# The combination of the attention groups, the split of its result, and the w_oa additions and splits made in two column halves

## The chip, the cores and the metric

The kernel runs on one core of one Trainium2 chip. The time is in device microseconds (us): one launch, from the core's start to its end, the median of several runs. The core has five engines that run side by side, each through its own instructions in order: PE (TensorE, the matrix products, with the weight loads PEld beside it), DVE (VectorE), ACT (ScalarE), POOL (GpSimd) and SP, which only issues DMAs in this kernel. A product lies in PSUM until another engine has read it; all else lies in SBUF or in DRAM.

## What is computed

One layer of a decoder trunk for 1024 prompt rows and 32 sample rows, 1056 columns in the kernel, which holds everything transposed (features on the 128 partitions, rows of the sequence along the columns). The part that matters here is the middle of the layer: three groups of attention heads are combined by softmax weights, the result goes through w_oa, a gated product, an addition to the other branch, and w_out.

```python
def combine_groups(outs, lses):
    w = jax.nn.softmax(jnp.stack(lses, axis=-1), axis=-1)
    o = jnp.sum(jnp.stack(outs, axis=-2) * w[..., None], axis=-2)
    return o.reshape(*o.shape[:-2], ATT_OUT_W)
...
    att = combine_groups(outs, lses).astype(h.dtype)
    yb, vrows = sgu_branch(uv, sgu_ln_g, sgu_ln_b, sgu_ws, sgu_b)
    mix = (jax.nn.sigmoid(ga) * (att @ w_oa) + jax.nn.sigmoid(gb) * (yb @ w_ob)) @ w_out
    h = layer_norm(ALPHA * h + mix, ln2_g, ln2_b)
    h = layer_norm(ALPHA * h + 0.5 * swiglu(h, f2_w1, f2_w3, f2_w2), ln3_g, ln3_b)
```

`att` has 256 features, `yb` 512, `mix` 1024. Before and behind this part stand two large feed-forward blocks, which take most of the time and which the change does not touch.

## The kernel before

**Products.** Every large product is made three times (`mm3`): an operand x is split into a rounded high part and the rest (`split`: an ACT cast for the high part, a DVE subtraction for the low one, lines 252 and 253), and hi·hi, hi·lo and lo·hi are added up in PSUM. A block is 128 output features by 264 columns (C); the 1056 columns are four blocks, c = 0 to 3. Of the PSUM banks three carry the tag `mm`. Each block in the part around the change takes one of the three, and the bank comes free when DVE has multiplied the block into its place (line 1581, in `product`; I call this the clearing of a block). So PE can be two to three blocks ahead of DVE and then stands.

**The stage.** `mix` (from line 1564) first makes `local(n)` for n = 0 to 5: block row n of the w_ob product, four blocks of 12 matmuls, each cleared by a DVE multiplication with a gate. Meanwhile generators run in the background: `attend` (scores, softmax, values), after it `combine` for head pair 0 and then 1, and `sample_join`, which combines the three groups for the 32 sample rows. Then `split_att` splits the two attention tiles, and the loop over n = 0 to 7 makes the w_oa products: four blocks of 6 matmuls each, cleared the same way, then the addition of both branches (line 1688), then the split of the sum into `m2[n]`, with the last `local` calls and three gates put between. Last comes w_out, whose block (0, c) needs all eight `m2`.

**Combination.** `combine` works out three rows of weights, writes them to DRAM (`cD`, line 1354), and loads each one back, spread over 64 partitions per head (`load`, line 1350, two DMAs for one weight tile `cb`). The loop at line 1358 then multiplies each group's tile by its weights (line 1361) and adds it up (line 1363), whole tiles of 1024 columns on DVE.

**What sets the order.** The code is only the order of recording. A scheduler that simulates the engines decides in which order the instructions stand on each engine, so that a changed duration can move instructions that the diff does not name. A DMA waits in SP's queue behind the DMAs ahead of it, and a DVE instruction behind the DVE instructions ahead of it, whatever it needs itself.

Names in the profile: S, M, W, R, Q are pools of SBUF tiles (W holds split weights, R raw weights), `mm` and `ax` PSUM, `cD`, `jD`, `hD`, `zD` DRAM scratch. jD carries the sample rows' partial results to `sample_join`, hD the residual that w_out's blocks are added to, ws and st are a copy of a state that SP issues piece by piece. L109 on POOL is a one-column copy with which a fresh tile is taken.

## Time and profile before

| What | before |
|---|---|
| median of 3 runs | 2155.13 us |
| the runs | 2155.13, 2155.13, 2161.53 us |
| the profiled execution | 2158.47 us |
| its span (first to last instruction) | 2156.7 us |
| PE busy in the span | 2124.5 us |
| DVE busy | 1552.1 us |
| ACT busy | 889.5 us |
| POOL busy | 323.5 us |
| mean granted clock of PE | 0.995 |

The span is the time from the first to the last instruction of the profiled execution; 1.8 us lie around it (2158.47 less 2156.7). An engine's busy time is the union of its instructions. Times in the views below are microseconds from the start of the span. In a timeline a row gives start, length, engine, line, operation, tiles and sizes, the count of merged instructions, and in brackets how long the engine stood idle before it and what ended that.

### The profile page before, as it was taken

Reading aid. Unit: us, or ns where it says so; the run is one execution under the profiler, and the core shown is the slowest. Engines: PE = TensorE matmul, PEld = TensorE weight load, DVE = VectorE, ACT = ScalarE, POOL = GpSimd, SP = SyncE. Lnnn points to the kernel's source line nnn. Section 1 sums busy time; section 2 is a strip of 40 time slices with the busy share of each in tenths; the row PEclk is TensorE's granted clock in tenths of the full one; section 3 lists DMA queues with packets and bytes.
Section 4 is the critical chain, followed back from the end, with each engine's and each line's share of the span. In section 5 each row is a group of like instructions: output and inputs, shape, how many; then the busy total and the mean of one; then the engine's idle time right before and its main releaser. Section 6 shows DMA issues by size and latency. Waiting matters only on the chain.

```text
span 2156.7 us, 43261 instructions
## 1 busy us (share of the span) xinstructions
PE 2124.5 (99%) x17307; PEld 2086.6 (97%) x17307; DVE 1552.1 (72%) x2727; ACT 889.5 (41%) x1680; POOL 323.5 (15%) x249
## 2 busy tenths in 40 slices
PE   9999999999999999999999999999999999999997
PEld 8999999999999999999988889999999999999997
DVE  8876767747789834887766758787667767657887
ACT  5444444422124644334375544264444444421224
POOL 0432322200000012223000000000323333100000
PEclk9999999999999999999999999999999999999998
DMA  4444545598884335676865755423454544596852
GB/s 154 146 139 170 184 164 169 190 345 311 326 327 167 130 113 174 196 237 207 281 220 164 230 176 189 154 100 119 140 178 149 190 165 159 194 408 267 310 185 81
DMA packets 168378, 426.51 MB, mean 198 GB/s; under 512 B 24353, under 2 KB 59793, under 8 KB 165489
## 3 DMA queue, kind: packets, MB, share of 16 engines
q1 hardware_dynamic: 167744, 423.21, 56.4%
q8 instruction: 135, 2.21, 0.4%
q10 hardware_dynamic: 432, 0.54, 0.1%
q14 instruction: 67, 0.54, 0.1%
HBM read 304.31 MB, written 165.57 MB: 218 GB/s over the span
## 4 chain that ended last, share of the span: by engine, by line
PE 85%; DVE 5%; DMA 5%; issue 1%; POOL 1%; ACT 1%; SPq 1%; ACTq 0%; DVEq 0%; POOLq 0%
PE ax L241 44%; PE mm L241 37%; DMA M<-kv 2%; PE ax L1205 1%; DVE W L253 1%; PE ax L1252 1%; DMA R<-wz 1%; PE ax L1229 1%; DVE M L1428 1%; DMA S<-zD 1%; DMA S<-cD 1%; DVE X L1433 0%; DVE S L631 0%; DMA S<-hD 0%; PE ax L620 0%
## 5 line engine op out<-in xcount | busy, mean ns | idle before, releaser
L241 PE MATMUL mm<-S,W 128*128 128x264 f32 x5400 | 715.7, 287 | 7.9 <-ACT S L252 2.6
L241 PE MATMUL ax<-S,W 128*128 128x264 f32 x5400 | 706.7, 284 | 0.7 <-ACT S L1033 0.5
L241 PEld LDWEIGHTS mm<-S,W 128*128 128x128 f32 x5400 | 677.6, 189 | 21.6 <-issue 8.5
L241 PEld LDWEIGHTS ax<-S,W 128*128 128x128 f32 x5400 | 676.3, 188 | 3.5 <-ACT S L1033 1.7
L241 PE MATMUL ax<-S,S 128*128 128x264 f32 x3240 | 475.7, 284 | 1.8 <-ACT S L1033 1.7
L241 PEld LDWEIGHTS ax<-S,S 128*128 128x128 f32 x3240 | 427.7, 188 | 2.4 <-ACT S L1033 1.9
L241 PE MATMUL mm<-S,S 128*128 128x264 f32 x2280 | 359.6, 286 | 2.7 <-DVE S L924 2.7
L241 PEld LDWEIGHTS mm<-S,S 128*128 128x128 f32 x2280 | 311.3, 189 | 4.1 <-ACT M L593 2.2
L252 ACT CAST W<-R 128x256 fp32r<-128x256 f32 (+2 forms) x175 | 130.7, 764 | 309.3 <-PE mm L241 140.1
L385 POOL TENSOR_TENSOR Q<-R 128x512 f32<-128x512 f32 x49 | 69.9, 1428 | 797.7 <-DMA R<-w13b 219.9
L253 DVE TENSOR_TENSOR W<-R,W 128x256 fp32r<-128x256 f32 (+2 forms) x175 | 156.8, 899 | 22.4 <-ACT W L252 21.4
L252 ACT CAST W<-Q 128x1024 fp32r<-128x1024 f32 (+1 forms) x78 | 76.8, 984 | 218.6 <-POOL Q L386 88.0
L819 DVE SCALAR_TENSOR_TENSOR S<-ax,S 128x264 f32<-128x264 f32 x240 | 99.3, 427 | 66.8 <-PE ax L241 66.4
L461 DVE TENSOR_TENSOR S<-ax,M 128x264 f32<-128x264 f32 x82 | 32.6, 432 | 148.7 <-PE ax L241 148.7
L253 DVE TENSOR_TENSOR S<-Q,S 128x1024 fp32r<-128x1024 f32 (+1 forms) x78 | 111.3, 1427 | 5.5 <-ACT S L252 5.4
L109 POOL CAST S<-ones 128x1 fp32r<-128x1 f32 x36 | 13.6, 384 | 676.0 <-PE ax L241 414.0
L253 DVE TENSOR_TENSOR W<-Q,W 128x1024 fp32r<-128x1024 f32 (+1 forms) x78 | 90.3, 1158 | 29.0 <-ACT W L252 28.9
L252 ACT CAST S<-Q 128x1024 fp32r<-128x1024 f32 (+1 forms) x78 | 76.7, 984 | 67.8 <-PE ax L241 47.2
L253 DVE TENSOR_TENSOR S<-S,M 128x528 fp32r<-128x528 f32 x72 | 83.9, 1165 | 3.7 <-ACT M L252 2.4
L386 POOL TENSOR_TENSOR Q<-Q,R 128x512 f32<-128x512 f32 x49 | 82.7, 1688 | 2.7
L252 ACT CAST S<-R 128x512 fp32r<-128x512 f32 (+1 forms) x62 | 41.9, 676 | 94.2 <-DMA sumsA<-S 39.6
L393 POOL TENSOR_TENSOR Q<-R,Q 128x512 f32<-128x512 f32 x49 | 80.2, 1637 | 1.2
(209 smaller groups left out, 2051.1 us busy)
## 6 DMA issues: line engine op xcount, KB each, us to landing
ws<-st SPq DMA_DIRECT2D x144, 256.0 KB
S<-sumsA SPq DMA_DIRECT2D x63, 528.0 KB
S<-sumsB SPq DMA_DIRECT2D x63, 528.0 KB
M<-kv SPq DMA_DIRECT2D x96, 256.0 KB
sumsA<-M SPq DMA_DIRECT2D x90, 264.0 KB
sumsB<-M SPq DMA_DIRECT2D x90, 264.0 KB
R<-w13b SPq DMA_DIRECT2D x44, 512.0 KB
R<-w13a SPq DMA_DIRECT2D x42, 512.0 KB
```

The source lines that it names most:

```text
L241: mm = lambda a, b, s, e: nc.tensor.matmul(o, a[:, cc], b, start=s, stop=e, skip_group_check=True)
L252: a = self.nc.scalar.copy(hi, src)
L253: b = self.nc.vector.tensor_tensor(lo, src, hi.bitcast(F32), op=ALU.subtract)
L385: tt(s12[:, lo], cd[:, lo], cd[:, hi], op=ALU.add)
L386: tt(s12[:, hi], s12[:, lo], ab[:, lo], op=ALU.subtract)
L393: tt(s34[:, hi], ab[:, hi], s12[:, hi], op=ALU.subtract)
L461: go(one, 5, False, lambda x: tt(h[:, x, 1], one[x], p7[:, x], op=ALU.add))
L819: nc.vector.scalar_tensor_tensor(y(x, r, e), bank[x], HALF, y(x, r, e), op0=ALU.mult, op1=ALU.add)
L1205: nc.tensor.matmul(pS[h][:, r, :nk], q[e, i * P : (i + 1) * P], k[e, k0 : k0 + nk], start=True, stop=True)
L1229: nc.tensor.transpose(pT[r][:, h, o], s[:, r, h, o], self.ident)
L1252: nc.tensor.matmul(pv[0][e, (i % 4) * P : (i % 4 + 1) * P], V[:, i - (nb - 1) + b, e], sT[:, r, h, b * P : b * P + P], start=b == 0, stop= ...
L1428: nc.vector.tensor_tensor(t, t, p.unsqueeze(1).to_broadcast(t.shape), op=ALU.mult)
```

## The change

Three edits, all to operations on whole columns. In `combine` the multiplication and the addition are made in two instructions each, columns 0 to 511 and 512 to 1023. In `split_att` the 1024 prompt columns are split in two halves. In the w_oa loop the addition and the split are made as two halves of 528 columns, each half added and then split; the two tiles of `m2` are taken ahead of the addition. No matmul, no DMA and no tile is added or left out.

```diff
@@ combine
         for g in range(3):
             aT = self.attT.pop((hp, g))
             load(g + 2)
-            nc.vector.tensor_tensor(aT, aT, cbs.popleft(), op=ALU.mult)
-            if g:
-                nc.vector.tensor_tensor(att[:, :NP], att[:, :NP], aT, op=ALU.add)
+            cb = cbs.popleft()
+            for o in (slice(0, 512), slice(512, NP)):
+                nc.vector.tensor_tensor(aT[:, o], aT[:, o], cb[:, o], op=ALU.mult)
+            for o in (slice(0, 512), slice(512, NP)) if g else ():
+                nc.vector.tensor_tensor(att[:, o], att[:, o], aT[:, o], op=ALU.add)
             yield
@@ split_att
-                for o in (slice(0, NP), slice(NP, NT)):
+                for o in (slice(0, 512), slice(512, NP), slice(NP, NT)):
                     self.split(h[:, o], l[:, o], self.att[hp][:, o])
@@ the w_oa loop of mix
-            nc.vector.tensor_tensor(mt[n], mt[n], ta[n], op=ALU.add)
             m2.append((self.S([P, NT], F32R), self.S([P, NT], F32R)))
-            self.split(*m2[n], mt[n])
+            for o in (slice(0, NT // 2), slice(NT // 2, NT)):
+                nc.vector.tensor_tensor(mt[n][:, o], mt[n][:, o], ta[n][:, o], op=ALU.add)
+                self.split(*(x[:, o] for x in m2[n]), mt[n][:, o])
```

The scheduler's order moves with it. In the changed program the lines behind line 1363 have other numbers: 1361 is now 1363, 1363 is 1365, and 1448, 1452, 1581, 1645 and 1647 are each two higher; 1688 is 1692.

**DVE, the combination of head pair 1.** First the order before, from the subtraction of a w_ob weight (L253 on W) on. L1581 clears a block, L1361 and L1363 are the combination, L1459, L1461 and L1464 belong to `sample_join`.

```order
L253 TENSOR_TENSOR W_15517<-R_15516,W_15517 128x512
L1459 TENSOR_SCALAR X_15497<-M_15392,X_15489 128x64
L1581 TENSOR_TENSOR S_15104<-S_15104,mm_15522 128x264
L1461 SCALAR_TENSOR_TENSOR X_15497<-M_15392,X_15489,X_15497 128x64
L1361 TENSOR_TENSOR S_15061<-S_15061,S_15298 128x1024
L1461 SCALAR_TENSOR_TENSOR X_15497<-M_15392,X_15489,X_15497 128x64
L1581 TENSOR_TENSOR S_15104<-S_15104,mm_15536 128x264
L1361 TENSOR_TENSOR S_14348<-S_14348,S_15302 128x1024
L1464 COPY X_15497<-X_15497 128x64
L1581 TENSOR_TENSOR S_15104<-S_15104,mm_15550 128x264
L1363 TENSOR_TENSOR S_15061<-S_15061,S_14348 128x1024
L1581 TENSOR_TENSOR S_15104<-S_15104,mm_15564 128x264
```

And the changed program, from the last clearing ahead of the same subtraction on (S_15107 is the row of blocks that S_15102 was, S_15109 the row that S_15104 was).

```order
L1583 TENSOR_TENSOR S_15107<-S_15107,mm_15512 128x264
L253 TENSOR_TENSOR W_15527<-R_15526,W_15527 128x512
L1363 TENSOR_TENSOR S_15066<-S_15066,S_15303 128x512 x2
L1583 TENSOR_TENSOR S_15109<-S_15109,mm_15532 128x264
L1363 TENSOR_TENSOR S_14348<-S_14348,S_15307 128x512 x2
L1583 TENSOR_TENSOR S_15109<-S_15109,mm_15546 128x264
L1365 TENSOR_TENSOR S_15066<-S_15066,S_14348 128x512
L1583 TENSOR_TENSOR S_15109<-S_15109,mm_15560 128x264
L1365 TENSOR_TENSOR S_15066<-S_15066,S_14348 128x512
L1363 TENSOR_TENSOR S_14724<-S_14724,S_15329 128x512 x2
L1454 TENSOR_REDUCE X_15500<-M_15402 128x1
L1583 TENSOR_TENSOR S_15109<-S_15109,mm_15574 128x264
```

The first multiplication by the weights now stands one clearing earlier: before, block 0 of the row S_15104 was cleared ahead of it, now its counterpart comes behind it. `sample_join`, whose first instruction is L1454 (1452 before), has moved from ahead of the combination into it.

**SP, the loads of the same combination.** Before:

```order
L1438 DMA jD<-X_13031 128x66
L1448 DMA M_15392<-jD 64x66 x2
L231 DMA R_15578<-wo 128x512
L1354 DMA cD<-S_14961 16x128 x3
L1350 DMA S_15298<-cD 64x1024 x2
L1350 DMA S_15302<-cD 64x1024 x2
L231 DMA R_15650<-wo 128x512
L1350 DMA S_15324<-cD 64x1024 x2
```

And the changed program:

```order
L1440 DMA jD<-X_13031 128x66
L1450 DMA M_15402<-jD 64x66
L231 DMA R_15588<-wo 128x512
L1354 DMA cD<-S_14966 16x128 x3
L1350 DMA S_15303<-cD 64x1024 x2
L1350 DMA S_15307<-cD 64x1024 x2
L1350 DMA S_15329<-cD 64x1024
L231 DMA R_15660<-wo 128x512
L1350 DMA S_15329<-cD 64x1024
L1450 DMA M_15402<-jD 64x66
```

The last load of jD, which `sample_join` needs, now goes behind all the weight loads of the combination; one half of the third weight tile goes ahead of a w_ob load.

**DVE, the start of the w_oa loop.** L1647 (1649) is a row sum of a w_out tile, L1470 (1472) puts the sample rows into the attention tiles, L253 on W is the low part of the first two w_oa weights. Before:

```order
L1647 TENSOR_REDUCE X_15604<-Q_15606 128x8
L1581 TENSOR_TENSOR S_15232<-S_15232,mm_15701 128x264
L253 TENSOR_TENSOR W_15716<-R_15715,W_15716 128x256
L1581 TENSOR_TENSOR S_15721<-S_15721,mm_15748 128x264
L1581 TENSOR_TENSOR S_15721<-S_15721,mm_15756 128x264
L1581 TENSOR_TENSOR S_15721<-S_15721,mm_15764 128x264
L1581 TENSOR_TENSOR S_15721<-S_15721,mm_15772 128x264
L253 TENSOR_TENSOR W_15740<-R_15739,W_15740 128x256
L1688 TENSOR_TENSOR S_14895<-S_14895,S_15721 128x1056
```

And the changed program:

```order
L1649 TENSOR_REDUCE X_15614<-Q_15616 128x8
L1583 TENSOR_TENSOR S_15237<-S_15237,mm_15711 128x264
L1472 COPY S_13970<-ax_15608 64x32 x2
L1472 COPY S_15066<-ax_15608 64x32 x2
L253 TENSOR_TENSOR W_15726<-R_15725,W_15726 128x256
L253 TENSOR_TENSOR S_15738<-S_13970,S_15737 128x32
L253 TENSOR_TENSOR S_15746<-S_15066,S_15745 128x32
L1583 TENSOR_TENSOR S_15731<-S_15731,mm_15762 128x264
L1583 TENSOR_TENSOR S_15731<-S_15731,mm_15770 128x264
L1583 TENSOR_TENSOR S_15731<-S_15731,mm_15778 128x264
L1692 TENSOR_TENSOR S_14900<-S_14900,S_15731 128x528
L1583 TENSOR_TENSOR S_15731<-S_15731,mm_15786 128x264
```

The copies and splits of the sample rows, done long before in the old order, now stand directly around the low part of the first w_oa weight; the addition's first half stands ahead of the fourth clearing.

## The prediction

> **What bounds the kernel now.** I read the page first, then PE's own timeline through the stage of the change, then DVE and SP beside each gap that PE shows there. The first part of the page settles the scale:

> ```profile
> PE 2124.5 (99%) x17307; PEld 2086.6 (97%) x17307; DVE 1552.1 (72%) x2727; ACT 889.5 (41%) x1680; POOL 323.5 (15%) x249
> ```

> PE is busy 2124.5 us of a span of 2156.7 us, and the change takes no matmul away. It can win only stalls of PE, 32 us in the whole kernel, and of these only the ones in its own stage. PE's timeline from the last `local` rows to the first w_out block:

> ```profile
> 1263.08 22.10 PE L241 MATMUL mm<-S,W 128*128 128x264 f32 x180
> 1286.59 1.70 PE L241 MATMUL mm<-S,W 128*128 128x264 f32 x12 [1.40 <-DVE S L1581]
> 1288.83 0.30 PE L1467 MATMUL ax<-ident,X 128*128 128x128 f32 x1 [0.54 <-DVE X L1464]
> 1289.07 3.19 PE L241 MATMUL mm<-S,W 128*128 128x264 f32 x24
> 1292.91 1.74 PE L241 MATMUL mm<-S,W 128*128 128x264 f32 x12 [0.65 <-DVE S L1581]
> 1295.44 6.09 PE L241 MATMUL mm<-S,W 128*128 128x264 f32 x48 [0.79 <-DVE S L253]
> 1302.07 35.27 PE L241 MATMUL mm<-S,W 128*128 128x264 f32 x282 [0.54 <-ACT W L252]
> 1337.80 19.03 PE L241 MATMUL mm<-S,W 128*128 128x264 f32 x150 [0.46 <-DVE S L1581]
> 1357.22 2.96 PE L241 MATMUL mm<-S,W 128*128 128x264 f32 x22 [0.38 <-DVE S L1707]
> ```

> The brackets are the stalls: 1.40 + 0.54 + 0.65 + 0.79 + 0.54 + 0.46 + 0.38 = 4.76 us. The unstalled rate is 22.10 / 180 = 0.123 us per matmul, so 12 matmuls (one block of `local`) take 1.47. From 1302.07 to 1356.83 PE makes 432 matmuls in 54.76 us, where 432 x 0.123 is 53.1: some 1.7 us of stalls, 0.46 of them in a bracket, the rest too short for one. What holds PE at 1286.59 stands on DVE:

> ```profile
> 1279.39 0.43 DVE L1581 TENSOR_TENSOR S<-S,mm 128x264 f32<-128x264 f32 x1 [0.25 <-PE mm L241]
> 1280.86 0.42 DVE L1581 TENSOR_TENSOR S<-S,mm 128x264 f32<-128x264 f32 x1
> 1284.68 1.23 DVE L1361 TENSOR_TENSOR S<-S,S 128x1024 f32<-128x1024 f32 x1 [3.20 <-DMA S<-cD]
> 1286.02 0.42 DVE L1581 TENSOR_TENSOR S<-S,mm 128x264 f32<-128x264 f32 x1
> 1287.35 1.23 DVE L1361 TENSOR_TENSOR S<-S,S 128x1024 f32<-128x1024 f32 x1 [0.91 <-DMA S<-cD]
> 1288.60 0.42 DVE L1581 TENSOR_TENSOR S<-S,mm 128x264 f32<-128x264 f32 x1
> 1290.69 1.23 DVE L1361 TENSOR_TENSOR S<-S,S 128x1024 f32<-128x1024 f32 x1 [0.20 <-DMA S<-cD]
> 1292.43 0.42 DVE L1581 TENSOR_TENSOR S<-S,mm 128x264 f32<-128x264 f32 x1
> 1294.87 0.43 DVE L1581 TENSOR_TENSOR S<-S,mm 128x264 f32<-128x264 f32 x1
> ```

> L1361 at 1284.68 waits 3.20 us for its weights, and the next clearing waits behind it until 1286.02. PE had filled its three banks at 1263.08 + 22.10 = 1285.18 and stood until that clearing ended. The gaps at 1292.91 and 1295.44 end with the clearings of 1292.43 and 1294.87, which stand behind whole-tile operations. So what bounds this stretch is DVE's order around three arrivals of weights, 1284.68, 1287.35 and 1290.69, which the halves do not bring forward.

> **The price of a half.** A whole operation beside two halves of the same size:

> ```profile
> L1361 DVE TENSOR_TENSOR S<-S,S 128x1024 f32<-128x1024 f32 x6 | 7.4, 1226 | 8.0 <-DMA S<-cD 8.0
> 1215.18 1.28 DVE L1428 TENSOR_TENSOR M<-M,X 128x512 f32<-128x512 f32 x2
> L1688 DVE TENSOR_TENSOR S<-S,S 128x1056 f32<-128x1056 f32 x8 | 10.0, 1251 | 0.0
> ```

> Two of 512 take 1.28 us in a row, one of 1024 takes 1.23: a cut costs 0.05. The diff adds 28 DVE instructions (6 + 4 in the combination, 2 in `split_att`, 8 additions, 8 low parts), 1.4 us of DVE in all, and ten ACT casts. A clearing that comes just behind a started operation waits 0.6 us in place of 1.2.

> [...]

> **The combination of head pair 1, step by step.** The order moves L1361 (1363 now) ahead of one clearing, the one that stood at 1280.86. PE fills its banks one block sooner, at 1285.18 - 1.47 = 1283.71. Against that, the small operations of `sample_join` and its transpose on PE (the 0.54 gap) move behind, and the operations are halves. I take the arrivals 0.3 us later (the instructions ahead of L1341, which makes the weights, stand in another order; bounds 0 and 0.7, one weight subtraction more ahead of it, 676 ns in the rows below), 0.6 for a half, 0.4 for a clearing to its end, and 0.05 until PE goes on:

> - Weights at 1285.0, two halves, clearing ended 1286.6; PE restarts at 1286.65, a stall of 2.9 in place of 1.4, one block behind the old order.
> - Second weights at 1287.65, two halves, clearing ended 1289.25; PE at 1289.3. Behind it half an addition and a clearing, ended 1290.2, so the next block follows at once at 1290.75.
> - Half an addition, third weights at 1291.0, two halves, L1454, clearing ended 1292.75; PE at 1292.8.
> - A subtraction for a weight, half an addition, clearing ended 1294.3; PE at 1294.35 until 1295.8. Half an addition and two clearings are through by 1295.7; the last row of `local` runs without a stall, 48 matmuls, 1295.8 to 1301.7.

> Before, the same point is 1295.44 + 6.09 = 1301.53. So the block that is lost first is won back: **+0.2 us**. If nothing is won back it is +1.5; if the clearings slip in better than I count, the gaps 0.54 + 0.65 + 0.79 go too and it is -2.0.

> What must hold for this is that L1454 does not wait, for it now stands ahead of a clearing. Its operand comes by the last jD load:

> ```profile
> 1275.01 1.10 SPq L1448 DMA_DIRECT2D M<-jD  x2
> 1278.27 0.15 DVE L1452 TENSOR_REDUCE X<-M 128x1 f32<-128x3 f32 x1
> 1279.32 2.76 SPq L1350 DMA_DIRECT2D S<-cD  x4
> 1282.81 1.08 SPq L1350 DMA_DIRECT2D S<-cD  x2
> 1283.30 7.27 DMA S<-cD
> ```

> SP issues the last weights from 1283.30 on, and they land 7.27 us later. The last jD load goes out behind them, about 1284.0. With the 3.3 us that it took before (1275.01 to 1278.27) it is there at 1287, with 7.27 at 1291.3; L1454 is reached at 1292.2. So nothing, on the dearer row with 0.9 us to spare.

> **The start of the w_oa loop.** Its first weight takes the slot of the last `local` weight, an ACT cast (1301.61, the 0.54 us gap), and that stays. New is that the low part of this weight stands on DVE behind the copies of the sample rows:

> ```profile
> L1470 DVE COPY S<-ax 64x32 f32<-64x32 f32 x4 | 0.7, 187 | 0.1
> L1647 DVE TENSOR_REDUCE X<-Q 128x8 f32<-128x1024 f32 x5 | 6.1, 1211 | 0.0
> L253 DVE TENSOR_TENSOR W<-R,W 128x512 fp32r<-128x512 f32 x8 | 5.4, 676 | 0.2 <-ACT W L252 0.2
> 1301.61 0.40 ACT L252 CAST W<-R 128x256 fp32r<-128x256 f32 x1 [1.61 <-issue]
> ```

> PE has six matmuls (0.74 us) with the high part before it needs the low one. The transpose follows the last `local` block at 1301.7, the copies take 4 x 0.187 = 0.75 from about 1302.0, the subtraction 0.4: ready at 1303.2, needed at 1302.2 + 0.74 = 1302.95. **+0.3 us**, bounds 0 and 1.3 (a row sum of 1.21 that starts just before).

> **The w_oa blocks.** DVE is nearly full here (start and end, length, then busy time of PE, PEld, DVE, ACT and POOL, the granted clock, DMA):

> ```profile
> 1303.00:1338.00 35.00, 34.54 (x278) 33.82 (x277) 30.75 (x54) 13.79 (x20) 0.00 (x0) 1.00 0.58 189
> ```

> DVE is busy 30.75 of 35 us, PE 34.54. The 1.7 us of short stalls are clearings behind a row sum, an addition or a subtraction; halves cut the wait behind the latter two. Half of 1.7 would be -0.85; 16 cuts at 0.05 add 0.8 us of DVE and give some back. I take **-0.5 us**, bounds -1.7 and +0.8. ACT's casts in halves and two more table loads have cover: ACT is busy 13.79 of these 35 us. A table load is 1.28 us and stands on ACT where it idles for 5.21 and 7.31:

> ```profile
> 1285.27 0.62 ACT L252 CAST W<-R 128x512 fp32r<-128x512 f32 x1 [5.21 <-PE mm L241]
> 1293.19 0.22 ACT L252 CAST S<-S 128x32 fp32r<-128x32 f32 x1 [7.31 <-DVE S L1470]
> 1297.62 1.28 ACT L1684 ACT_TABLE_LOAD   x1 [1.18 <-DMA S<-zD]
> ```

> I cost them at 0; without that cover they would hold a weight's cast for up to 2.6 us.

> **The first w_out block and head pair 0.**

> ```profile
> 1350.31 0.33 SPq L220 DMA_DIRECT2D R<-wout  x1
> 1351.25 4.34 SPq L279 DMA_DIRECT2D S<-hD  x8
> 1356.73 0.43 DVE L1707 SCALAR_TENSOR_TENSOR S<-mm,S 128x264 f32<-128x264 f32 x1 [2.88 <-DMA S<-hD]
> 1212.83 0.44 PE L1229 MATMUL ax<-ident,S 128*128 128x128 f32 x2 [1.26 <-ACT S L1233]
> ```

> The hD loads stand in SP's queue behind the w_out load of 1350.31; in the new order one w_out load fewer is ahead of them. The 0.38 us stall at 1357.22 should go in the main: **-0.3 us** (0 to -0.4). The w_out load that goes behind them is for a later unit, and a unit is used for 4 x 24 matmuls, 11.8 us. For head pair 0 the stall of 1.26 ends when a whole multiplication has freed a tile; two halves are 0.05 later each time: **+0.1** (0 to 0.2).

> **The sum.** 0.2 + 0.3 - 0.5 - 0.3 + 0.1 = -0.2 us. On the profiled execution, whose span is 2156.7 us (2158.47 with what lies around it), that is 2156.5; the median of the runs lies 3.3 us under that execution, so I take 2155.13 - 0.2, rounded: **2155.0 us**. The forecast is no change that can be told: a difference under 0.3% (6.5 us) is about what a measurement of this kernel cannot tell from none, and the three runs are themselves 6.4 us apart.

> **The rivals.**

> *All clearings slip in.* The combination's gaps go (-2.0), the short stalls of w_oa (-1.7), 0.38 at w_out, and the 1.40 as well if the old count of clearings ahead of the weights hardly matters: -5.5, 2149.6 us. For it: every one of these gaps ends at DVE. Against it: one clearing fewer stands ahead of the wait, and arrivals set the pace. To pass 6.5 us it needs something outside this stage too.

> *The sample rows come late.* Place: L1454 on DVE, ahead of a clearing. If the last jD load is slower than I count, every microsecond past 1292.2 is one of PE, whose three banks are full. The longest wait for a load in the chain of waits is

> ```profile
> 1064.14 9.92 DMA S<-zD
> ```

> With 9.92 us it lands at 1293.9: +1.7, and with nothing won back in the combination (+1.5), the row sum in the way (+1.3) and a further +0.8 in w_oa 2160.4 us. It decides from a landing at 1292.2 on, and is slower beyond 0.3% from about 1298.5. For it: the load is now the last of its queue's ten rows shown above. Against it: it is 64 x 66 values and took 3.3 us.

> *DVE runs full.* At 88% busy each cut costs its whole fixed part, and the clearings queue. The dear price, the whole of 28 x (2 x 0.674 - 1.226) = 3.4 us by mean lengths, with the 0.5 not won, is 2158.8 us. [...] For it: DVE's 30.75 of 35. Against it: the pair of 512.

> **How the numbers follow.** The forecast has 0.60: 0.56 within the bound, 0.02 on either side by the runs' own spread. All clearings slip in: 0.16, of which 0.11 beyond the bound. Sample rows late: 0.12, 0.07 beyond, since its price is not bounded by a row of the same load. DVE full: 0.12, 0.05 beyond with the spread. Faster 0.02 + 0.11 = 0.13, slower 0.02 + 0.07 + 0.05 = 0.14, the same 0.73. The likeliest case's own range is 2153 to 2157 us from the bounds that add up by chance. The range of 8 in 10 reaches from the first rival, 2150, to the second, 2160.4, and to what a median takes from the upper run: 2150 to 2161.

> **What would show it.** In the changed profile: PE stalls 2 to 3.5 us once near 1284, ended by the clearing behind the first pair of halves (right), or under 1.5 (my count of clearings is wrong); PE begins the w_oa loop within 1 us of 1302; the low part of its first weight ends a PE gap of 0.2 to 0.5; the rows from there to the w_out block take 53.5 to 55 us; the gap ended by L1707 is gone. L1454 shows a DMA as its releaser if the second rival is right. A sum of DVE in the w_oa stretch over 33 of 35 us would speak for the third. The forecast fails if a stall appears in a part that the order leaves alone, or if the runs move as a whole by more than their spread.

## The result, and the profile after

| | before | after |
|---|---|---|
| median | 2156.23 us | 2159.89 us |
| runs | 22, from 2153.85 to 2161.53 | 22, from 2155.36 to 2164.74 |
| ratio | | 1.0014, 95% interval 1.0008 to 1.002 |
| the profiled execution's span | 2156.7 us | 2162.0 us |

The change makes the kernel slower by 0.14%, some 3 us: less than the 0.3% that I took for what can be told, but with 22 runs on either side it can be told. The forecast was no change (2155.0 us). The profiled execution of the changed kernel is the slowest of its 22 runs, so its stalls are larger than usual ones; the repeats below show how much larger.

The first part of the page of the changed kernel:

```profile
PE 2127.2 (98%) x17307; PEld 2089.4 (97%) x17307; DVE 1553.2 (72%) x2755; ACT 893.8 (41%) x1692; POOL 317.9 (15%) x249
```

The matmuls are the same in number, and PE is busy 2.7 us longer. DVE has the 28 instructions more that were counted, for 1.1 us more of busy time where I had worked out 1.4; ACT has two instructions more than the ten casts, the two table loads. PE's timeline through the stage, for the rows from 1263.08 on that were shown of before:

```profile
1264.26 8.97 PE L241 MATMUL mm<-S,W 128*128 128x264 f32 x72
1273.47 11.92 PE L241 MATMUL mm<-S,W 128*128 128x264 f32 x96 [0.24 <-DVE S L1583]
1287.55 2.12 PE L241 MATMUL mm<-S,W 128*128 128x264 f32 x12 [2.16 <-DVE S L1583]
1289.88 12.92 PE L241 MATMUL mm<-S,W 128*128 128x264 f32 x96 [0.22 <-DVE S L1583]
1302.64 0.27 PE L1469 MATMUL ax<-ident,X 128*128 128x128 f32 x1
1303.34 1.01 PE L241 MATMUL mm<-S,W 128*128 128x264 f32 x6 [0.43 <-ACT W L252]
1304.51 11.19 PE L241 MATMUL mm<-S,W 128*128 128x264 f32 x90 [0.16 <-DVE W L253]
1317.91 17.99 PE L241 MATMUL mm<-S,W 128*128 128x264 f32 x132 [2.22 <-DVE S L1583]
1336.32 6.84 PE L241 MATMUL mm<-S,W 128*128 128x264 f32 x54 [0.41 <-DVE S L1583]
1343.40 22.81 PE L241 MATMUL mm<-S,W 128*128 128x264 f32 x181 [0.25 <-DVE S L1583]
```

Up to the w_oa loop it reads as predicted: one long stall behind the first pair of halves (2.16 us), no gaps of 0.54, 0.65 and 0.79 behind it, and the loop begins 39.08 us behind the first `local` row (1303.34 - 1264.26), where before it was 38.99. New is the stall of 2.22 us at 1317.91, which the prediction does not have. Behind it the gap ended by L1707 is gone. Two more things are in the lengths: 12 matmuls take 2.12 us at 1287.55 (1.47 is the full rate), and 132 take 17.99 (16.2). Both rows stand behind a long stall, where the granted clock was 0.50 for 3.41 us. Here are the stretch with the second stall and the one behind it (start and end, length, then busy time of PE, PEld, DVE, ACT and POOL, the granted clock, DMA):

```profile
1315.97:1319.38 3.41, 1.47 (x12) 1.50 (x13) 2.64 (x5) 1.04 (x3) 0.00 (x0) 1.00 0.27 72
1319.38:1322.79 3.41, 3.41 (x17) 3.41 (x17) 3.13 (x7) 1.26 (x2) 0.00 (x0) 0.50 0.75 217
```

What stands ahead of 1317.91 on ACT of the changed kernel:

```profile
1315.12 1.08 ACT L1686 ACTIVATE S<-S 128x1056 f32<-128x1056 f32 x1 [5.85 <-DMA S<-zD]
1316.11 0.91 ACT L252 CAST W<-R 128x512 fp32r<-128x512 f32 x2
```

On its DVE:

```profile
1316.74 0.69 DVE L253 TENSOR_TENSOR W<-R,W 128x512 fp32r<-128x512 f32 x1 [2.77 <-ACT W L252]
1317.35 0.76 DVE L1583 TENSOR_TENSOR S<-S,mm 128x264 f32<-128x264 f32 x2
```

And in SP's queue, the load that the sigmoid needs:

```profile
1308.93 0.58 SPq L1141 DMA_DIRECT2D S<-zD  x1
```

ACT of the kernel before, at the same place:

```profile
1311.10 0.62 ACT L252 CAST W<-R 128x512 fp32r<-128x512 f32 x1 [2.63 <-PE mm L241]
1312.20 1.09 ACT L1684 ACTIVATE S<-S 128x1056 f32<-128x1056 f32 x1 [0.47 <-DMA S<-zD]
```

Read it from the last fence up. Before, ACT casts the last w_ob weight at 1311.10, 9.03 us into the w_oa loop, as soon as PE has left the slot, and then takes the sigmoid of the fifth gate, whose load from zD has just come. After, the two have changed places: ACT waits 5.85 us for that load (issued at 1308.93), and the cast stands behind it until 1316.11, 12.77 us into the loop. DVE waits 2.77 us for the cast, two clearings stand behind DVE's subtraction, and PE behind the clearings. Neither PE nor DVE waits for the sigmoid itself in this loop.

### The profile page after: what moved, and what is told of

Read it like the earlier page. It is cut to its first block, busy times and chain, and to the rows that moved or that the text cites. A ratio compares the mean times of both kernels' runs of the same rounds, so it can differ in the third digit from the quotient of the medians.

```text
span 2162.0 us, 43300 instructions
## 1 busy us (share of the span) xinstructions
PE 2127.2 (98%) x17307; PEld 2089.4 (97%) x17307; DVE 1553.2 (72%) x2755; ACT 893.8 (41%) x1692; POOL 317.9 (15%) x249
## 4 chain that ended last, share of the span: by engine, by line
PE 89%; DVE 4%; DMA 4%; ACT 1%; issue 1%; POOL 1%; SPq 0%; ACTq 0%; DVEq 0%; POOLq 0%
PE ax L241 46%; PE mm L241 38%; PE ax L1205 1%; DMA M<-kv 1%; DMA S<-zD 1%; PE ax L1252 1%; PE ax L1229 1%; DVE W L253 1%; DMA S<-cD 0%; DVE S L253 0%; DVE S L631 0%; DMA R<-wz 0%; DVE S L554 0%; PE ax L620 0%; PE ax L1549 0%
## 5 line engine op out<-in xcount | busy, mean ns | idle before, releaser
L241 PE MATMUL mm<-S,W 128*128 128x264 f32 x5400 | 719.0, 288 | 10.2 <-DVE S L1583 5.5
L241 PE MATMUL ax<-S,W 128*128 128x264 f32 x5400 | 706.6, 284 | 2.2 <-ACT S L1033 2.0
L241 PEld LDWEIGHTS mm<-S,W 128*128 128x128 f32 x5400 | 681.0, 190 | 23.9 <-issue 8.0
L241 PEld LDWEIGHTS ax<-S,W 128*128 128x128 f32 x5400 | 676.1, 188 | 5.0 <-ACT S L1033 3.4
L241 PE MATMUL ax<-S,S 128*128 128x264 f32 x3240 | 475.9, 284 | 2.9 <-ACT S L1033 1.8
L241 PEld LDWEIGHTS ax<-S,S 128*128 128x128 f32 x3240 | 427.6, 188 | 3.8 <-ACT S L1033 2.0
L241 PE MATMUL mm<-S,S 128*128 128x264 f32 x2280 | 359.4, 286 | 2.6 <-DVE S L924 2.6
L241 PEld LDWEIGHTS mm<-S,S 128*128 128x128 f32 x2280 | 311.0, 189 | 3.9 <-issue 2.9
L252 ACT CAST W<-R 128x256 fp32r<-128x256 f32 (+2 forms) x175 | 130.6, 764 | 305.7 <-PE mm L241 126.7
L253 DVE TENSOR_TENSOR W<-R,W 128x256 fp32r<-128x256 f32 (+2 forms) x175 | 155.7, 893 | 25.2 <-ACT W L252 24.1
L252 ACT CAST W<-Q 128x1024 fp32r<-128x1024 f32 (+1 forms) x78 | 76.8, 984 | 222.4 <-POOL Q L386 90.8
L253 DVE TENSOR_TENSOR S<-Q,S 128x1024 fp32r<-128x1024 f32 (+1 forms) x78 | 112.0, 1436 | 5.5 <-ACT S L252 5.5
L253 DVE TENSOR_TENSOR W<-Q,W 128x1024 fp32r<-128x1024 f32 (+1 forms) x78 | 89.9, 1153 | 31.1 <-ACT W L252 31.1
L252 ACT CAST S<-Q 128x1024 fp32r<-128x1024 f32 (+1 forms) x78 | 76.7, 984 | 68.2 <-PE ax L241 50.2
L253 DVE TENSOR_TENSOR S<-S,M 128x528 fp32r<-128x528 f32 x72 | 83.8, 1164 | 2.6 <-ACT M L252 1.0
L252 ACT CAST S<-R 128x512 fp32r<-128x512 f32 (+1 forms) x62 | 41.9, 676 | 99.9 <-DMA sumsA<-S 42.3
L393 POOL TENSOR_TENSOR Q<-R,Q 128x512 f32<-128x512 f32 x49 | 80.7, 1647 | 1.2
```

Source lines behind the costliest of these rows:

```text
L241: mm = lambda a, b, s, e: nc.tensor.matmul(o, a[:, cc], b, start=s, stop=e, skip_group_check=True)
L252: a = self.nc.scalar.copy(hi, src)
L253: b = self.nc.vector.tensor_tensor(lo, src, hi.bitcast(F32), op=ALU.subtract)
L393: tt(s34[:, hi], ab[:, hi], s12[:, hi], op=ALU.subtract)
```

## The experiments

Every comparison has 11 or 12 runs of the kernel against 23 to 35 of the kernel before on the same chip, so a ratio's interval is some 0.0008 to 0.0010 to either side. That is as large as the effect, so I read the traces beside it. In every profile I take three stretches, read at the same matmuls: **L** from the first local row (before: 1263.08) to the first w_oa block (1302.07), **W** from there to the matmul at 1337.80, **T** from there to 1400.09 in the w_out blocks. One table for all, in microseconds (in `after_early` the stall near 1285 is another one: PE's transposition waits there for L1466, a copy of the sample rows):

| kernel | stall near 1285 | granted clock behind it | L | W | T | ratio |
|---|---|---|---|---|---|---|
| before | 1.40 | 1.00 | 38.99 | 35.73 | 62.28 | |
| before_again | 1.12 | 1.00 | 38.04 | 35.59 | 62.67 | 0.9997 |
| comb_alone | 1.09 | 1.00 | 37.56 | 35.69 | 62.70 | 1.0002 |
| before_swap | 1.12 | 1.00 | 38.03 | 37.43 | 62.69 | 1.0008 |
| oa | 1.21 | 1.00 | 38.62 | 36.49 | 61.60 | 1.0001 |
| oa_tied | 1.27 | 1.00 | 38.18 | 35.68 | 61.61 | 0.9994 |
| oa_tied_again | 1.21 | 1.00 | 39.04 | 35.66 | 61.63 | 0.9986 |
| before_stall | 2.28 | 0.50 | 38.52 | 35.51 | 62.71 | 0.9997 |
| before_stall_fill | 1.30 | 1.00 | 38.11 | 36.41 | 62.53 | 1.0004 |
| splitatt_alone | 2.17 | 0.50, twice as long | 40.81 | 36.80 | 62.56 | 1.0006 |
| comb_split | 2.08 | 1.00 | 38.82 | 35.98 | 62.76 | 1.0010 |
| comb_split_again | 1.94 | 1.00 | 38.20 | 36.08 | 62.64 | 1.0012 |
| after_tied | 2.50 | 0.50 | 39.46 | 36.11 | 61.62 | 0.9997 |
| tied_again | 2.57 | 0.50 | 39.20 | 36.12 | 61.60 | 1.0010 |
| after | 2.16 | 0.50 | 39.08 | 40.07 | 61.61 | 1.0014 |
| after_again | 2.03 | 1.00 | 38.27 | 36.57 | 61.61 | 1.0009 |
| after_early | 2.09 | 0.50 | 39.30 | 35.67 | 61.65 | 1.0001 |
| after_late | 3.39 | 0.50 | 40.00 | 37.12 | 61.60 | 1.0007 |
| tied_late | 2.85 | 0.50 | 39.44 | 36.08 | 61.60 | 1.0003 |
| tied_fill | 1.15 | 1.00 | 39.34 | 35.98 | 61.61 | 1.0006 |

### The sigmoid ahead of the cast

Two kernels take the new order out and put it into the old kernel. The first is the changed kernel with the sigmoid issued behind the cast (three neighbours on DVE change places as well):

```diff
-                nc.scalar.activation(ta[n], ta[n], AF.Sigmoid)
+                with self.tc.issue_after(self.cast) if n == 4 else ExitStack():
+                    nc.scalar.activation(ta[n], ta[n], AF.Sigmoid)
```

Here `self.cast` is the cast of the last w_ob weight.

> The changed kernel with one order on ACT put back: the sigmoid of the fifth w_oa gate (n = 4) is issued behind the cast of the last w_ob weight, as before the change; every engine's order is otherwise that of the change but for three neighbouring swaps on DVE. Theory A (the sigmoid waits for its gate's load with the weight's cast queued behind it): PE's 2.2 us stall near 1318 is gone, the stretch from the first w_oa matmul to the first w_out clearing is 3 to 4 us shorter than in the changed kernel, ratio to before 0.999 to 1.0005. Rival B (28 more DVE instructions cost it, or the clearing that the combination lost): the stretch stays, ratio 1.001 to 1.002.

The second is the kernel before, whole operations throughout, with the fifth gate loaded and its sigmoid recorded in `local(6)`, and the last w_ob cast issued behind it:

```diff
+                if n == 6:
+                    early.append(self.fetch_z(30))
+                    sig = nc.scalar.activation(early[0], early[0], AF.Sigmoid).ins
```

> The kernel before, whole tiles everywhere, with that one order changed: the gate's sigmoid (n = 4) ahead of the cast of the last w_ob weight on ACT. Theory A: a PE stall of 1.5 to 3 us appears behind that cast, the sigmoid shows a DMA of zD as its releaser, ratio 1.001 to 1.002. Rival B: no stall, ratio 0.9995 to 1.0005.

Measured: 2156.84 us, ratio 0.9997 [0.9988, 1.0006] without the swap, and 2158.41, 1.0008 [1.0000, 1.0017] for the swap alone. W says the same: it falls from 40.07 to 36.11 without the swap, and rises from 35.6 or 35.7 to 37.43 with it. The stall of PE behind the cast is 0.92 us in `before_swap`, less than the 1.5 to 3 expected. Then the halves of the w_oa loop alone, which bring the swap with them, and the combination with `split_att` alone, which does not:

> Only the w_oa additions and splits in halves; the combination and its split whole. The sigmoid stands ahead of the cast here too. Theory A: the stall of about 2 us in the w_oa loop is there, ratio 1.0008 to 1.002, as the whole change. Rival B in the form of the combination's lost clearing: ratio 0.9995 to 1.0005.

> The combination and the split of its result in halves, the w_oa additions and splits whole. Here the sigmoid stays behind the cast. Theory A: ratio 0.9995 to 1.0005, PE begins the w_oa loop within 0.5 us of the kernel before when counted from the last local rows; no stall over 1 us from there to w_out. Rival B in the form of the lost clearing: 1.5 us later at the w_oa loop, ratio 1.0007 or more.

`oa`: 2156.57, 1.0001 [0.9992, 1.0009], under the 1.0008 or more that the swap was to give: W has the swap (36.49), but T is 1.0 us shorter. `comb_split`: 2159.47, 1.0010 [1.0001, 1.0018], which a swap that explains everything would not give. So the first four kernels show one cost, and that there is another.

The same four parts once more, and a kernel that loads the w_oa gates four ahead in place of three (`ta` begins with four), which puts the sigmoid behind the cast, the sample rows' operations ahead of the combination, and needs no more table loads, with all halves kept:

> The changed kernel itself once more, for a second profile. Theory A (the sigmoid in front of the weight's cast, priced by how late its gate's load lands): the stretch from the first w_oa matmul to the 282nd is as much over 36.1 us as the load of zD lands behind the time at which the weight's slot comes free, somewhere from 0.5 to 4 us; ratio 1.0005 to 1.002. Rival C (the 2.2 us stall of the first profile is a chance of that one execution and the change costs elsewhere): the stretch is at 36.1 and the ratio is still 1.001 or more.

> The changed kernel with the sigmoid behind the cast, once more. Theory A: ratio 0.999 to 1.0003, the stretch 36.0 to 36.3 us. Rival C: ratio 1.001 as the change.

> The combination and the split of its result in halves, once more, since its first ratio of 1.001 does not fit theory A while its profile shows no stall that the kernel before has not. Theory A: ratio 0.9995 to 1.0006. Rival D (the new order of the combination costs by itself, through the lost clearing and two more table loads): 1.0007 to 1.0015 again, and the last local rows or the head pair 0 part 0.7 us or more longer than before in its profile.

> All halves of the change, and each gate of the w_oa loop loaded one block row earlier (four ahead in place of three). The scheduler then puts the sigmoid behind the cast and the sample rows ahead of the combination again, as before the change. Theory A: no stall over 1 us in the w_oa loop, ratio 0.9985 to 1.0000. Rival B (the cuts cost by their number): 1.001 or more.

Measured: 2158.57, 1.0009 [1.0000, 1.0019]; 2158.44, 1.0010 [1.0001, 1.0018]; 2158.71, 1.0012 [1.0003, 1.0021]; 2156.00, 1.0001 [0.9992, 1.0010]. Note `tied_again`: the kernel whose first measurement was 0.9997 is 1.0010 here. One measurement of this size settles nothing. `comb_split_again` repeats the cost, but its profile shows neither longer last local rows (L 38.20) nor a longer head pair 0, as its expectation asked. `after_early` has all the halves, W at 35.67 and a ratio of 1.0001, which speaks against a cost by the number of halves.

SP and then ACT of `after_again` show why the swap's price differs from one execution to the next:

```profile
1304.57 0.58 SPq L1141 DMA_DIRECT2D S<-zD  x1
```

```profile
1308.80 1.09 ACT L1686 ACTIVATE S<-S 128x1056 f32<-128x1056 f32 x1 [3.90 <-DMA S<-zD]
1309.79 0.60 ACT L252 CAST W<-R 128x512 fp32r<-128x512 f32 x1
```

Here the load is there 4.2 us after its issue (1304.57 to 1308.80), in `after` 6.2 us. The cast stands 10.83 us into the loop (1309.79 - 1298.96), 1.8 us later than in its own place, and PE has cover for most of that: its timeline has only a gap of 0.27 there. In `after`, the cast is 3.7 us late and PE stands for 2.22. In W the swap costs 0.5 us (`after_again`), 0.8 (`oa`), 1.0 (`after_late`), 1.8 (`before_swap`) and 4.0 (`after`), against the same order without it: 1.6 on average. Two of these are not the swap alone. In `after`, the 132 matmuls behind the stall take 17.99 us where `after_again` takes 16.43 for the same row, and these 1.56 us are the half clock that followed. In `before_swap`, 0.87 us are the gap ahead of the matmul at which W ends, and that gap is anything from 0.22 to 1.10 us in the kernels with whole w_oa operations. Without `after` the average is 1.0.

### Each edit alone, and no edit

> The kernel before under a name of its own: nothing is changed. It tells how far a kernel without any change may fall from the runs beside it. If the differences of 1.0008 to 1.0012 seen so far come from the changes, this one lies between 0.9995 and 1.0005, and from the start of the stage's last 950 us (PE's block at 1195 us) to the end its trace shows 946 us, as the first trace of before does (946.0). If it falls outside 0.9993 to 1.0007, such differences cannot be told from no change at all, and the theories of a lost clearing and of a late load have nothing left to explain.

> Only the multiplications and additions of combine are halved; split_att and the w_oa loop are as before. The order keeps the first multiplication behind the same clearing, the sample rows' operations ahead of the combination and the sigmoid behind the last weight cast. If the halves in combine are what costs (their own 0.05 us per cut, or the small shifts on PE and ACT in head pair 0), 1.0010. If the cost comes from the order that split_att brings with it, 1.0000, with PE's stall near 1285 still 1.4 us or less.

> Only the split of the attention tiles is made in halves (two casts and two subtractions more); the multiplications are whole. The order puts the first multiplication one clearing earlier, the sample rows' operations behind it, the last load of jD behind the weight loads of the combination, and two more ACT table loads. If this order is what costs, 1.0010 (about +2 us) with a PE stall of 2 to 3 us near 1285. If the order costs nothing and the halves in combine do, 1.0000.

> Only the w_oa blocks' additions and splits are halved, and the sigmoid of the fifth gate is issued behind the cast of the last w_ob weight, as before. If the halves of the w_oa loop win the 0.5 us of the stall ahead of w_out and the swap with the sigmoid was all that they cost, 0.9997, with the stretch from the first w_oa block to the second at 35.7 to 36.1 us. If the swap costs nothing on the whole time, the same as with the swap, 1.0001.

Measured: 2156.74, 0.9997 [0.9989, 1.0006]; 2157.08, 1.0002 [0.9993, 1.0010]; 2158.08, 1.0006 [0.9998, 1.0015]; 2156.28, 0.9994 [0.9986, 1.0002]. The unchanged kernel under another name is off by 0.0003, but the two measurements of `after_tied` and `tied_again` are 0.0013 apart, so a difference of 0.0010 is read only where it repeats over several kernels. The halves in `combine` alone cost nothing that can be told. It is the halves in `split_att`, which no term of my sum named, that bring the new order around the combination: with them alone the first multiplication stands ahead of the clearing, the sample rows behind it, and the stall is 2.17 us. And the w_oa halves, once the swap is out, are a gain. PE of `oa_tied` in the w_oa loop:

```profile
1300.74 28.18 PE L241 MATMUL mm<-S,W 128*128 128x264 f32 x228 [0.54 <-ACT W L252]
1329.33 6.82 PE L241 MATMUL mm<-S,W 128*128 128x264 f32 x54 [0.41 <-DVE S L1581]
1336.42 28.76 PE L241 MATMUL mm<-S,W 128*128 128x264 f32 x230 [0.27 <-DVE S L1581]
```

228 matmuls run without a bracket, 54 and 230 more follow with small gaps ahead of them, and the stall ahead of w_out that ended at L1707 is not there. T is 61.60 to 61.65 in every kernel with these halves, and 62.28 to 62.76 in every one without.

### The stall near 1285, and the clock behind it

The table shows a pattern: where the stall was 2.09 us or longer, the granted clock was 0.50 for the next 3.4 us. Four kernels were to tell whether the second cost is this stall, the half clock, or the sample rows. The first is the kernel before with nothing added but the stall; two instructions change places on DVE:

```diff
+            with self.tc.issue_after(self.first_mult) if held else ExitStack():
                 with self.urgent():
                     nc.vector.tensor_tensor(t[:, cc], t[:, cc], p, op=ALU.mult)
```

`held` is true for block row 3, c = 0, and `first_mult` is the first multiplication of head pair 1.

> The kernel before, in which one clearing and the first multiplication of the second combination change places on DVE (nothing is halved; the multiplication by the first weights is issued ahead of the clearing of block row 3, c = 0). Theory of the clock: PE's stall grows from 1.1 to 1.4 us to about 2.7 us, that is more than half of a stretch of 3.4 us, and in about two of three executions the granted clock is 0.5 in the next 3.4 us; the mean clock over the runs falls by 0.0005 and the time is 1.0007 to 1.0012. Theory of the lost clearing alone: the stall grows as well but is won back within the next blocks, time 1.0000 to 1.0004, mean clock as in the kernel before. Theory of the sample rows (their late operations, the late jD load, two more table loads are what costs): they are untouched here, so 1.0000.

The second fills the stall with nine matmuls that are made twice:

```diff
+            for k, (xh, xl) in enumerate(xs[:fill]):
+                self.mm3(p, wo, k * P, xh[:, cc], xl[:, cc], k == 0, False)
```

> As the run before it, but nine of the twelve matmuls of block row 3, c = 2 are made twice (the first time for nothing, into the same bank), so that PE works 1.1 us of its stall. The scheduler moves three neighbours on DVE and one cast. Theory of the clock: the stall is 1.6 us, under half of a stretch of 3.4 us, the clock stays 1.00, and the kernel is faster than the one with the bare stall by 0.0004 to 0.0008 although it makes more matmuls. Theory of the lost clearing alone, and that of the sample rows: the same time as with the bare stall.

The third and fourth are the changed kernel, and the one without the swap, with the first multiplication put behind that clearing:

> The changed kernel, in which the first multiplication goes back behind the clearing of block row 3, c = 0; all halves, the sample rows' place, the late jD load, the table loads and the sigmoid ahead of the weight cast stay. Theory of the clock and of the clearing: PE's stall near 1285 is 1.1 to 1.4 us again, no half clock there, and 1.0003 (what is left is the sigmoid, about +1.3 us, less what the w_oa halves win, about 1). Theory of the sample rows: as the changed kernel, 1.0010.

> The changed kernel with both orders put back: the first multiplication behind the clearing, the fifth gate's sigmoid behind the weight cast. Theory of the clock, the clearing and the sigmoid together: all that costs is gone, what the w_oa halves win is left, 0.9995. Theory of the sample rows: 1.0005 (about +2 us from them, less 1).

Measured: 2156.41, 0.9997 [0.9988, 1.0005]; 2158.14, 1.0004 [0.9995, 1.0012]; 2159.12, 1.0007 [0.9998, 1.0017]; 2158.20, 1.0003 [0.9994, 1.0011]. PE of `before_stall`, and two of its stretches (start and end, length, then busy time of PE, PEld, DVE, ACT and POOL, the granted clock, DMA):

```profile
1281.14 4.72 PE L241 MATMUL mm<-S,W 128*128 128x264 f32 x24 [2.28 <-DVE S L1584]
1285.70 0.27 PE L1469 MATMUL ax<-ident,X 128*128 128x128 f32 x1
1285.73 10.47 PE L241 MATMUL mm<-S,W 128*128 128x264 f32 x84
1296.74 35.29 PE L241 MATMUL mm<-S,W 128*128 128x264 f32 x282 [0.54 <-ACT W L252]
```

```profile
1278.26:1281.68 3.42, 1.14 (x9) 0.93 (x9) 2.10 (x4) 0.00 (x0) 0.00 (x0) 1.00 1.02 252
1281.68:1285.09 3.41, 3.41 (x18) 3.41 (x18) 3.38 (x6) 0.62 (x1) 0.00 (x0) 0.50 1.03 299
```

The stall is there, the half clock is there, and L is 38.52 all the same, between the two profiles of before. The stall is 0.9 us longer than in the first profile of before, and 24 matmuls take 4.72 us in place of 2.95, but DVE goes on meanwhile, and when the clock is back it is so far ahead that the three gaps are gone and 84 matmuls run in a row. In this profile the lost clearing is won back, as the prediction had it: what the half clock takes, PE would else have stood in the gaps. The time, 0.9997, did not bear out the theory of the clock, which had 1.0007 or more. It does not refute it either: that theory also had the mean granted clock 0.0005 lower, and over the 11 runs it is 0.9955, as in the runs of the kernel before beside them, so the half clock need not have come in most of them. `before_stall_fill` keeps the full clock and has L 0.4 us shorter (38.11), but W is 36.41 and the time 1.0004. The theory of the clock had it faster than the bare stall, and missed.

The third and fourth kernels did not do what they were for; `after_late` shows why. With the first pair of halves behind the clearing, both pairs stand ahead of the next clearing, and PE waits for the second weights in place of the first:

```profile
1273.24 13.40 PE L241 MATMUL mm<-S,W 128*128 128x264 f32 x108 [0.24 <-DVE S L1586]
1290.03 13.46 PE L241 MATMUL mm<-S,W 128*128 128x264 f32 x96 [3.39 <-DVE S L1586]
```

They say only that this one move does not take the stall out of this order.

What the half clock does in the changed order can be read from `after` and `after_again`, one program whose profiles differ in the clock. DVE of `after`, then of `after_again`, at the same clearings:

```profile
1295.03 0.94 DVE L1583 TENSOR_TENSOR S<-S,mm 128x264 f32<-128x264 f32 x2
1299.91 0.43 DVE L1583 TENSOR_TENSOR S<-S,mm 128x264 f32<-128x264 f32 x1 [0.58 <-PE mm L241]
```

```profile
1291.39 0.76 DVE L1583 TENSOR_TENSOR S<-S,mm 128x264 f32<-128x264 f32 x2
1295.53 0.43 DVE L1583 TENSOR_TENSOR S<-S,mm 128x264 f32<-128x264 f32 x1 [0.34 <-PE mm L241]
```

`after` is 3.64 us behind `after_again` at the first of the two, as it was at the second weights (3.66), and 4.38 at the second, where DVE waits for PE. So here it is PE that falls 0.7 us behind, and the half clock accounts for it: the 96 matmuls from 1289.88 on in `after` need 11.8 us at the full rate and lose half of the 2.19 us up to the clock's return at 1292.07, 12.9 together, and they take 12.92; in `after_again` the same row takes 12.20. In `splitatt_alone`, where the half clock lasted twice as long, it takes 14.50. Of the 0.81 us by which L is longer in `after`, 0.7 are this.

The runs point the same way. Each run has its mean granted clock on record, and one stretch of half clock takes 0.0008 off it (half of 3.41 us in 2157). In all six repeats and parts with the changed order (`after_again`, `after_tied`, `tied_again`, both of `comb_split`, `splitatt_alone`; one run of `after_again`, recorded at 0.946, left out) it is 0.0002 to 0.0007 lower on average than in the runs of the kernel before beside them, in the six with the old order (`before_again` to `oa_tied_again` in the table) from 0.0004 lower to 0.0005 higher. So more half clock comes with the changed order, and the two profiles of `comb_split`, both at the full clock near 1285, need not be typical of its runs.

The last two kernels fill the stall in the changed order (six matmuls made twice, without the swap), and repeat the part that wins:

> The changed kernel with the sigmoid tied behind the weight cast, in which six of the twelve matmuls of block row 3, c = 2 are made twice, so that PE works 0.74 us of its stall near 1285. Theory of the half clock: the two profiles of this kernel without the six showed stalls of 2.50 and 2.57 us, the granted clock at about 0.6 behind them, and 39.46 and 39.20 us from the first local block behind 1260 to the first w_oa block. With the six the stall is 1.8 us, the clock there stays 1.00 and the stretch is 38.3 to 38.6 us, although PE makes more matmuls; the time is 0.9995 to 1.0000. Theory of the lost clearing and the late sample rows without the clock: the stretch stays at 39.2 to 39.5 us, or grows by what the neighbours moved on DVE cost.

> Only the w_oa blocks' additions and splits halved, with the fifth gate's sigmoid behind the weight cast, once more: 0.9994 to 0.9997 if the 1.0 us that the traces show at the second w_oa row and the first w_out blocks is the whole effect; 1.0000 if the first measurement was chance.

Measured: 2158.42, 1.0006 [0.9998, 1.0015], and 2154.74, 0.9986 [0.9975, 0.9996]. PE of `tied_fill`:

```profile
1272.95 12.64 PE L241 MATMUL mm<-S,W 128*128 128x264 f32 x102 [0.24 <-DVE S L1585]
1286.74 1.73 PE L241 MATMUL mm<-S,W 128*128 128x264 f32 x12 [1.15 <-DVE S L1585]
1289.16 1.70 PE L241 MATMUL mm<-S,W 128*128 128x264 f32 x12 [0.68 <-ACT W L252]
1291.72 10.34 PE L241 MATMUL mm<-S,W 128*128 128x264 f32 x81 [0.87 <-DVE S L1585]
...
1303.08 28.51 PE L241 MATMUL mm<-S,W 128*128 128x264 f32 x228 [0.54 <-ACT W L252]
```

The clock stays full (12 matmuls in 1.70 and 1.73), and L is 39.34 all the same, where the theory of the half clock had 38.3 to 38.6: two smaller gaps stand where the half clock was. So L can be long without the half clock. The scheduler had moved some of DVE's neighbours for this kernel, so it is not a clean test. `oa_tied` is faster than the kernel before in both its measurements, by 1.4 us the first time (within its interval) and by 3.1 the second (beyond it, and more than the 1.0 us that the traces show); it is the best version found, and faster than the changed kernel.

## Why the prediction was wrong, point by point

The sum was 0.2 + 0.3 - 0.5 - 0.3 + 0.1 = -0.2 us. By the traces it is:

| step | predicted | traces |
|---|---|---|
| combination of head pair 1 (L) | +0.2 | +0.8 |
| start of the w_oa loop (W, without the swap) | +0.3 | +0.4 |
| ACT in the w_oa loop: the swap (W) | 0 | +1.6 |
| w_oa halves and first w_out block (T) | -0.8 | -1.0 |
| head pair 0 | +0.1 | 0.0 |
| sum | -0.2 | +1.8 |

L is 39.12 on average over the seven profiles with the changed order whose stall was left as it came (`after`, `after_again`, `after_tied`, `tied_again`, both of `comb_split`, `splitatt_alone`), and 38.35 over the seven with the old (`before` to `oa_tied_again` in the table). Head pair 0 is the stretch from 1195.10 to 1263.08: 67.75 on average in the kernels with halves in `combine`, 67.70 in the others. The medians say +3.7 and, on the repeat, +1.9 us; the sum of the traces lies at the lower of the two (at +1.2 with 1.0 for the swap, as without `after`), and what is over is within what two measurements of one kernel differ by (`after_tied` and `tied_again`: 0.0013, or 2.8 us).

The ratios can be set against each other in the same way, kernels with a thing against kernels without it, two measurements of one kernel averaged. The swap: `after` against `after_tied`, `oa` against `oa_tied`, `before_swap` against `before_again`, +0.0008 to +0.0011, or 1.7 to 2.4 us. The order around the combination, with the start of the w_oa loop: `after` against `oa`, `after_tied` against `oa_tied`, `comb_split` and `splitatt_alone` against `before_again` and `comb_alone`, +0.0009 to +0.0014, 1.9 to 2.9 us. The w_oa halves: `after_tied` against `comb_split`, `oa` against `before_swap`, `oa_tied` against `before_again` and `comb_alone`, -0.0007 to -0.0010, -1.5 to -2.0 us. Every ratio has an interval of some 0.0009 to either side, so these are estimates; but they agree with each other, and by them the combination's order costs about as much as the swap, and more than the 1.2 us that L and W show of it.

**The step that failed** is "ACT's casts in halves and two more table loads have cover ... I cost them at 0". I asked whether ACT has time for more instructions. It has, and no PE wait is seen behind the two table loads: the one at 1291.32 of `after` stands in an idle ACT. What I did not ask is in which order ACT does the old ones. The halves of the w_oa loop let the scheduler put the sigmoid ahead of the last weight cast, and an engine that idles is a full engine as long as its first instruction waits for a load: ACT of `after` stood for 5.85 us with the cast behind the sigmoid. I showed the moves on DVE and SP, and left the ACT order unread in the one stretch where a weight's cast and a load meet. The sentence's own price without cover, 2.6 us, lies among the delays of the cast that were measured, 1.7 to 3.7 us, but by luck, since it was the price of two table loads; `after_tied` and `before_swap` show the mechanism from both sides. So the term that stood at 0 measured +1.0 to +1.6 us in W and 1.7 to 2.4 by the ratios.

**The combination: mechanism right, size off.** This is the second term that failed. First restart 23.29 us behind the first local row (1287.55 - 1264.26), predicted 23.57; a stall of 2.16 ended by the clearing behind the first pair of halves, predicted 2 to 3.5; the small gaps gone. L at +0.2 held in the three profiles that kept the full clock (38.27, 38.82, 38.20: 38.43 on average, +0.1) and not in the others (39.08 to 40.81). I had the lost clearing won back always, at the full clock. What took its place, in `after` against `after_again` and in `splitatt_alone`, is the half clock behind the longer stall, 0.7 us for one stretch of it. It is not the whole: in `before_stall` a stall with half clock is won back in the old order, `tied_fill` has a long L without it, and in `after_tied` and `tied_again` PE also restarts 0.4 us later than in `after` (23.64 and 23.72). What the ratios show beyond L and W stays open.

**The w_oa loop** begins with a gap of 0.43 and one of 0.16 ended by the low part of its first weight (predicted 0.2 to 0.5): right, +0.4.

**The w_oa halves** were taken at -0.5 and the gap ahead of w_out at -0.3; T shows -1.0 for both. The sum is right in sign and nearly in size, but partly by luck: of the 432 matmuls from which the -0.5 was to come, the first 282 gain nothing (W is 35.68 and 35.66 in the two profiles of `oa_tied`, 35.73 and 35.59 in those of before), and most of the gain is the gap ended by L1707, which is 0.38 in the profile that I had, 0.61 to 0.83 in every other kernel with whole w_oa operations, and gone with the halves.

**Rivals.** The sample rows were not late, as DVE of `after` shows:

```profile
1291.20 1.29 DVE L1363 TENSOR_TENSOR S<-S,S 128x512 f32<-128x512 f32 x2
1292.40 0.15 DVE L1454 TENSOR_REDUCE X<-M 128x1 f32<-128x3 f32 x1
1292.47 0.42 DVE L1583 TENSOR_TENSOR S<-S,mm 128x264 f32<-128x264 f32 x1
```

L1454 follows its neighbour without a wait, 28.1 us behind the first local row, where I had it at 29.1. DVE did not run full: the price of this rival, the part of an instruction's length that halving its columns does not halve, was 2 x 0.674 - 1.226 = 0.12 us a cut, from mean lengths before (674 ns for 512 columns at L1428, 1226 for 1024 at L1361), and in `after` the 28 instructions add 1.1 us to DVE's busy time, 0.04 each; `oa_tied` has 16 of the cuts and wins, and in the first 35 us of the w_oa loop DVE is busy 27.9 us in `after` and 31.6 in `after_tied`, under the 33 that were to speak for this rival. That all clearings slip in is half true in `before_stall`, and not in the changed order. The case that came, a third engine's order, was not among the rivals; it is of the kind that the prediction named last, a stall "in a part that the order leaves alone", except that the order did not leave it alone.

## What to carry to other kernels

Where a scheduler decides, read the order of every engine in every stretch that the change touches, and look in it for an instruction that waits for a load and has moved ahead of one that somebody needs soon: a busy share, however low (ACT's 13.79 of 35 us here), does not price that. Cutting an operation in two is cheap where the pieces lie between clearings (0.06 us a cut in `after`: the pair at 1291.20 took 1.29 us, the whole before 1.23), and what it does to the order can cost more than it wins, so it is worth tying the one or two instructions that must not change places and measuring again. An effect of 0.1% wants an unchanged kernel under its own name beside it and the same stretch read from several profiles, since one trace holds one landing of each load.

## What the runs showed of the hardware

A stall of 2.16 us in `after` was followed by 3.41 us of PE at a granted clock of 0.50; one of 2.03 us in `after_again` was not. Two stretches each of `after` and of `after_again`, in the columns explained above:

```profile
1285.26:1288.68 3.42, 1.26 (x11) 1.14 (x10) 2.21 (x4) 0.00 (x0) 0.00 (x0) 1.00 1.02 230
1288.68:1292.09 3.41, 3.19 (x15) 2.91 (x15) 3.41 (x8) 1.39 (x2) 0.00 (x0) 0.50 1.13 389
```

```profile
1282.61:1286.02 3.41, 1.74 (x12) 1.53 (x12) 2.78 (x7) 0.38 (x1) 0.00 (x0) 1.00 1.07 262
1286.02:1289.44 3.42, 3.22 (x25) 3.10 (x26) 3.42 (x9) 1.82 (x3) 0.00 (x0) 1.00 1.00 369
```

What a half clock costs depends on what PE would have done in that time. In `before_stall` it took the place of gaps in which PE would have waited for DVE, and L shows no cost; in `after` it took 0.7 us in L and 1.56 in W.

The other thing was how far one load of 128x1056 varies: from its issue to the sigmoid that waited for it 4.2 us in `after_again` and 6.2 us in `after`, in the same order. With the sigmoid in its old place, behind the cast, the 282 matmuls of the stretch run in one row in the first profile of before.
